# A tanh-gelu MLP in Strassen form: weight casts on another engine, sums of the next weights split over two pairs, one split and an input cast a pair later

## The chip, the cores and the metric

The kernel runs on one core of a Trainium2 chip. The metric is the device time of one execution in microseconds (us). A core has five engines that run side by side: TensorE (PE, the matmuls; its weight loads are shown as PEld), VectorE (DVE), ScalarE (ACT), GpSimd (POOL) and SyncE (SP). SP only issues transfers (DMA); POOL issues some as well. Each engine works through its own instructions in order, and semaphores tie the engines together. SBUF is the on-chip memory, PSUM the eight banks that PE writes to.

## What is computed

For x of 8 x 1024 x 1024, w1 of 1024 x 4096 and w2 of 4096 x 1024, all float32:

```python
h = x @ w1
h = 0.5 * h * (1 + np.tanh(np.sqrt(2 / np.pi) * (h + 0.044715 * h ** 3)))
return (h @ w2).astype(np.float32)
```

The kernel multiplies in float16 and adds up in float32.

## The kernel before

The rows of x are taken in eight blocks of 1024 (`sb` 0 to 7). For each block `matmul1` computes the hidden values with the gelu, and a second routine multiplies them by w2: `matmul2_made` for blocks 0 and 1, `matmul2` for the rest. Both products use Strassen's scheme in Winograd's form: each operand is cut in two by two blocks named "11", "12", "21" and "22", seven products replace eight, and some operands are sums of blocks. For the weights these are `W_SUM`: sum 5 is "12" less "11", 6 is "22" less sum 5, 7 is "22" less "12", 4 is "21" less sum 6. For x they are `S_SUM`, of which sums 5, 7, 6 and 3 are made in that order. DVE makes all of them (line 119, the helper `tt`).

`matmul1` runs over eight pairs of columns of hidden values, j = 0 to 7. In a pair, product 1 and product 2 come first, then the late product 4 of the pair before, then 5, 6, 3 and 7, each for two columns (h = 0, 1) with four matmuls per column, all at line 435. PSUM banks are copied to SBUF by ACT (`act_copy`, line 135), DVE adds another bank to the copy, ACT applies the gelu (line 448). A bank that takes a second product must have been copied first, and those copies stand on ACT in order with the gelus.

Most instructions are held in the order in which the program is written (`keep_in_program_order`), so the place of a call in these loops is its place in its engine's queue.

Weights of w1 come in quarters of four columns (class `MadeQuad`). In block 0 each is loaded in float32 by SP into a ring of four staging buffers (`gc`), cast to float16 (`raw`), summed, and stored for later blocks. POOL casts the second and later quarters (lines 138 and 213 to 226 for casts and stores). Pair 0 is special (class `First`): its columns are multiplied plainly in eight products, the second half of the rows in two parts of 256. Of the first quarter, DVE casts columns 0 and 1 (line 196), and POOL casts columns 2 and 3, for pair 1, with the same line. The loads and the casts of these are kept in `self.more`, and the casts are issued at the end of `pair`. The sums of x are made after each part (`sums`), and then `matmul1` makes the four weight sums for columns 2 and 3. At pair 1 the sums of the second quarter are `jobs`: `half` is how many of them run ahead of products 5 and 6 on DVE, and the rest run at the pair's end.

In block 1 the weight sums are made again, now with a further level: `split_in_m1` loads parts of w2's blocks 2 and 3 into two `gc` buffers, makes four sums in two more of them, and POOL stores these (`in_d`, line 841). The four splits are loaded at the end of pairs 0 to 3, and `matmul1` takes their sums into the jobs of the next pair. Also in block 1, `steady` casts the next block's x: POOL copies two elements of a gelu result as a mark (`pace`, line 412), and then issues two transfers that cast x rows to float16 in DRAM (`xb`, line 407). SP later loads `xb` transposed.

The second product of blocks 0 and 1 runs over four row groups for each of seven products, with 16 matmuls each (line 933). `FILL` says which sums DVE makes after which group. In block 0 the parts "12" and "22" of w2 are loaded in float32 to staged buffers and cast by ACT; POOL stores `in_d` (line 820) and the results (line 671).

Of the kernel before, what the change touches and what calls it, by code (L numbers as in the profile page):

```python
# [61 lines left out]
def kernel(  # L62
# [7 lines left out]
    nc = tc.nc  # L70
# [38 lines left out]
    def psum():  # L109
        return pp.tile([P, HT], F32, name="ps")  # L110
# [33 lines left out]
    def columns(t, c, n=1):  # L144

        h, c = divmod(c, 2)
        return t[:, h * KH:(h + 1) * KH, c * P:(c + n) * P]
# [11 lines left out]
    class MadeQuad:  # L159


        def __init__(self, q, first, store):
            self.q, self.first, self.store = q, first, store
            self.raw = {b: unit(2 * KH, 2 * P) for b in BLOCKS}
            self.ops = {m: self.raw[b] for m, b in W_TERM.items()}
            if not first:
                for b in ("12", "11", "22", "21"):
                    nc.sync.dma_start(out=flat(self.raw[b]), in_=raw_d[q][:, BLOCKS.index(b), :])
# [127 lines left out]
    def x_blocks():  # L296
        return {b: unit(KH, HT) for b in ("22", "21", "12", "11")}

    def keep_clock(bank, n):

        for _ in range(n):
            tc.keep_in_program_order(
                nc.tensor.matmul(bank, lhsT=idle[:, :P], rhs=idle, start=True, stop=True)
            )

    class First:


        def __init__(self):
            self.identity = consts.tile([P, P], DT, name="identity")  # L310
            make_identity(nc, self.identity)
            self.idle = psum()
            keep_clock(self.idle, 7)
            self.xs = XOps(x_blocks())
            self.rows = {}
            for q in range(NQ):
                self.load(0, q)
            self.quad = MadeQuad(0, True, False)
            casts = [self.quad.load_cols(b, 0, 2, nc.vector.tensor_copy) for b in range(2)]
            for q in range(NQ):  # L320
                self.load(1, q)
            for q in range(NQ):
                self.cast(0, q)
                self.transpose(0, q)
                keep_clock(self.idle, 2)
            for cast in casts:
                cast()
            self.more = [self.quad.load_cols(b, 2, 2, nc.gpsimd.tensor_copy) for b in range(2)]

        def load(self, a, q):  # L330
            r0 = a * HT + q * P
# [3 lines left out]
        def cast(self, a, q):  # L335
            xn = tp.tile([P, 2, HT], DT, name="tmp")
            tc.keep_in_program_order(nc.vector.tensor_copy(out=xn, in_=self.rows[a, q]))
            self.rows[a, q] = xn
# [21 lines left out]
        def pair(self, gelu):  # L360


            def plain(bank, a, b, c, part=None):
                cols = slice(None) if part is None else slice(part * HT // 2, (part + 1) * HT // 2)
                for r in (1, 2):
                    w = columns(self.quad.raw[f"{r}{b}"], c)
                    for k in range(KH):
                        tc.keep_in_program_order(nc.tensor.matmul(  # L368
                            bank[:, cols], lhsT=w[:, k, :], rhs=self.xs.blocks[f"{a}{r}"][:, k, cols],
                            start=r == 1 and k == 0 and not part,  # L370
                            stop=r == 2 and k == KH - 1,
                            skip_group_check=bool(part),
                        ))

            def sums(h):
                for m in (5, 7, 6, 3):
                    self.xs.make(m, cols=slice(h * HT // 2, (h + 1) * HT // 2), pin=True)

            for q in range(3):
                self.cast(1, q)  # L380
            for b, c in ((1, 0), (1, 1), (2, 0), (2, 1)):
                bank = psum()
                plain(bank, 1, b, c)
                if b == 2:
                    self.transpose(1, c)
                gelu(f"1{b}", c, bank)
            self.cast(1, 3)
            self.transpose(1, 2)
            banks = {(c, b): psum() for c in range(2) for b in (1, 2)}
            for part in range(2):  # L390
                for c in range(2):
                    for b in (1, 2):
                        plain(banks[c, b], 2, b, c, part)
                        if part:
                            gelu(f"2{b}", c, banks[c, b])
                    if c == 0 and not part:
                        self.transpose(1, 3)
                sums(part)
            for casts in self.more:
                casts()  # L400

    def x_cast(s, after, rows=range(0, SB, P), xb=None):
        if xb is None:
            xb = xdram.tile([SB, H], DT, name="xb")
        with tc.issue_after(after.ins):
            for q in rows:
                nc.gpsimd.dma_start(out=xb[q:q + P, :], in_=x2[s * SB + q:s * SB + q + P, :])
        return xb

    def x_cast_paced(s, g_chunk, q, xb):  # L410

        mark = nc.gpsimd.tensor_copy(out=pace, in_=g_chunk[:, :2])  # L412
        return x_cast(s, mark, range(q * P, (q + 2) * P, P), xb)

    def x_transpose(xb, dma, blocks=None, which=range(4)):
        blocks = blocks or x_blocks()
        for b, t in [list(blocks.items())[i] for i in which]:
            a, k = int(b[0]) - 1, int(b[1]) - 1
            for j in range(KH):
                dma(  # L420
                    t[:, j, :],
                    xb[a * HT:(a + 1) * HT, (k * KH + j) * P:(k * KH + j + 1) * P],
                    transpose=True,
                )
        return blocks
# [3 lines left out]
    def matmul1(xs, sb, quads, start=None):  # L429
        g = {b: gp.tile([P, NI, HT], GT, name=f"g{b}") for b in ("11", "12", "21", "22")}  # L430
# [68 lines left out]
        def ahead(j):  # L499

            if sb > 1 or j // 2 == NI // QC - 1:
                return ()
            q, second = divmod(j, 2)
            if not second:
                quad = MadeQuad(q + 1, sb == 0, sb == 1)
                quads.append(quad)
                if sb == 0:
                    quad.load()
                    quads[q].keep_raw()
            quad = quads[q + 1]  # L510
            if sb == 0:
                return [lambda m=m: quad.sum(m, pin=True) for m in SUMS] if second else ()
            jobs = [lambda m=m: quad.sum(m, pin=True) for m in ((7, 4) if second else (5, 6))]
            if sb == 1:
                if second:
                    jobs += [lambda m=m: quad.inner_sums(m) for m in INNER_1]
            return jobs

        def steady(j):

            if 0 < sb < NSB - 1:
                when = (0, 1, 2, 3) if sb > 1 else (4, 5, 6, 7)
                if j in when:
                    nxt["xb"] = x_cast_paced(sb + 1, g["11"][:, 2 * j + 1, :], 2 * when.index(j), nxt.get("xb"))
                if j == 3 and sb > 1:
                    nxt["blocks"] = x_blocks()
                if j > 3 and sb > 1:
                    x_transpose(nxt["xb"], load_in_order, nxt["blocks"], range(j - 4, j - 3))
            if sb > 1 and j == 5:
                early[7] = gcp.tile([P, NI // 2, HT // 2], GT, name="gc")  # L530
                u, v = (inner_block(g["22"], b) for b in ("11", "21"))
                nc.gpsimd.tensor_tensor(out=early[7], in0=u, in1=v, op=SUB)  # L532

        nxt, early = {}, {}
        splits = []
        late = None
        pending = []
        for j in range(NI // 2):
# [13 lines left out]
            jobs = list(ahead(j))  # L552
# [33 lines left out]
            difference(j - 1)  # L586
            half = (len(jobs) + 1) // 2
            if start is not None and j == 1:
                half = 0
            if sb == 1:  # L590
                half = 3 if j % 2 else 0
                jobs += splits
                splits = []
            for job in jobs[:half]:
                job()
            def six(h):
# [62 lines left out]
            if sb == 1 and j < 2 * len(SPLIT_IN_M1):  # L659
                splits = split_in_m1(SPLIT_IN_M1[j // 2], j % 2)  # L660
            steady(j)
        difference(NI // 2 - 1)
        blocks = nxt.get("blocks")
# [183 lines left out]
    def inner_block(t, b):  # L847
        a, k = int(b[0]) - 1, int(b[1]) - 1
        return t[:, k * NI // 2:(k + 1) * NI // 2, a * HT // 2:(a + 1) * HT // 2]
# [171 lines left out]
    for sb in range(NSB):  # L1021
        g, early, nxt = matmul1(xs, sb, quads, first if sb == 0 else None)
# [36 lines left out]
```

## Time and profile before

| what | value |
|---|---|
| median of 5 runs | 1495.36 us (1494.83 to 1498.94) |
| the profiled execution | 1496.6 us |
| its span, first to last instruction | 1494.8 us |
| PE busy in the span | 1480.8 us (99%) |
| DVE, ACT, POOL busy | 1155.3, 609.7, 235.3 us |
| granted PE clock, mean | 0.997 |
| POOL casts at line 196 | 4, mean 1148 ns |
| ACT casts of the same shape from SBUF (line 135) | 16, mean 1045 ns |
| DVE sums of 128x1024 f16 (line 119) | 52, mean 814 ns |
| DVE sums of 128x2048 f16 | 88, mean 1261 ns |
| block 0: first product, second product | to 119.1 us, to about 215.8 us |
| block 1: first product, second product | to 314.5 us, to about 411.4 us |

The times in the table are from one profiled execution, except for the median. A row of the profile names the engine, the line, the tile written and read, the shape, the count, and how long the engine was idle before it and what released it. "DMA share" is the mean busy share of the 16 DMA engines; it can go a little over 1. The granted clock is the share of full speed that PE is given.

### The profile page before, as it was taken

What the parts mean: (1) busy time and instruction counts of PE and PEld (TensorE: products, weight loads), DVE (VectorE), ACT (ScalarE), POOL (GpSimd) and SP (SyncE); (2) the same over time, 40 slices, a digit from 0 to 9 for tenths busy, and PEclk for the clock granted to TensorE, in tenths of its full rate; (3) what the DMA queues carried; (4) which work ended last, traced back from release to release, by engine and by line L of the source; (5) the groups of instructions that cost most, each with busy time, mean ns of one, the idle gap of its engine ahead of it and who ended that gap; (6) DMA issues with size and microseconds to landing.
All of it is one profiled execution on the core that took longest, in us unless ns stands there. A gap on an engine that the chain in (4) does not pass through costs nothing.

```text
span 1494.8 us, 26327 instructions
## 1 busy us (share of the span) xinstructions
PE 1480.8 (99%) x9879; PEld 965.3 (65%) x9879; DVE 1155.3 (77%) x1792; ACT 609.7 (41%) x1146; POOL 235.3 (16%) x314
## 2 busy tenths in 40 slices
PE   8999999999999999999999999999999999999998
PEld 4444444444455788557875588755886568855687
DVE  6756548757767899778987799877997779877787
ACT  4566116531066411663126631366214652156510
POOL 3552022312311011110121001210011101101011
PEclk9999999999999999999999999999999999999999
DMA  9999996997997999999999899998999999997886
GB/s 331 329 342 395 261 339 224 384 286 246 345 318 183 327 296 309 333 225 367 305 323 315 226 381 311 303 321 241 358 297 315 309 262 339 294 367 243 293 282 214
DMA packets 242719, 453.70 MB, mean 304 GB/s; under 512 B 80672, under 2 KB 85792, under 8 KB 241696
## 3 DMA queue, kind: packets, MB, share of 16 engines
q1 hardware_dynamic: 215680, 358.69, 71.4%
q0 software_dynamic: 26912, 93.34, 21.3%
q8 instruction: 77, 1.26, 0.3%
q14 instruction: 50, 0.41, 0.1%
HBM read 355.47 MB, written 111.15 MB: 312 GB/s over the span
## 4 chain that ended last, share of the span: by engine, by line
PE 86%; issue 7%; DMA 3%; DVE 2%; POOL 2%; ACT 0%; POOLq 0%; DVEq 0%; ACTq 0%
PE ps L435 44%; PE ps L892 34%; PE ps L933 7%; DVE tmp L119 1%; DVE u L119 1%; DMA in_d<-gc 1%; DMA u<-in_w_dram 1%; PE ps L368 1%; DMA xb<-in_x_dram 1%; POOL out_dram L671 0%; POOL w_d L213 0%; POOL in_d L841 0%; PE ps L345 0%; DMA u<-in_x_dram 0%; POOL in_d L226 0%
## 5 line engine op out<-in xcount | busy, mean ns | idle before, releaser
L435 PE MATMUL ps<-u 128*128 128x512 f16 (+1 forms) x4104 | 750.0, 345 | 7.7 <-DVE u L119 3.5
L119 DVE TENSOR_TENSOR tmp<-tmp,ps 128x256 f32<-128x256 f32 (+1 forms) x930 | 450.6, 532 | 267.0 <-PE ps L435 174.3
L435 PEld LDWEIGHTS <-u 128*128 128x128 f16 x4104 | 402.0, 98 | 353.2 <-issue 17.5
L135 ACT COPY tmp<-ps 128x512 f32<-128x512 f32 x410 | 231.8, 582 | 309.3 <-PE ps L435 157.3
L448 ACT ACTIVATE g<-tmp 128x512 f16<-128x512 f32 x378 | 238.3, 633 | 170.6 <-DVE tmp L119 170.5
L892 PE MATMUL ps<-u,gc 128*128 128x256 f16 x2688 | 300.4, 273 | 0.0
L892 PEld LDWEIGHTS <-gc 128*128 128x128 f16 x2688 | 262.5, 98 | 31.2
L119 DVE TENSOR_TENSOR u<-u 128x2048 f16<-128x2048 f16 (+3 forms) x292 | 224.8, 809 | 16.8 <-DMA in_d<-u 7.3
L892 PE MATMUL ps<-u,g 128*128 128x256 f16 x2016 | 227.9, 273 | 0.0
L135 ACT COPY u<-ps 128x512 f32<-128x512 f32 (+1 forms) x134 | 78.0, 587 | 348.8 <-PE ps L892 341.3
L892 PEld LDWEIGHTS <-g 128*128 128x128 f16 x2016 | 197.3, 98 | 24.1
L683 POOL DMA_DIRECT2D out_dram<-u x70 | 64.1, 982 | 710.1 <-issue 365.7
L119 DVE TENSOR_TENSOR u<-u,ps 128x512 f32<-128x512 f32 x216 | 147.8, 684 | 34.6 <-PE ps L892 28.8
L933 PE MATMUL ps<-u,g 128*128 128x512 f16 x768 | 166.4, 379 | 0.0
L933 PEld LDWEIGHTS <-g 128*128 128x128 f16 x768 | 75.1, 98 | 90.7
L119 DVE TENSOR_TENSOR g<-g,g 128x2048 f16<-128x2048 f16 (+1 forms) x136 | 130.7, 983 | 1.6 <-ACT g L448 1.6
L119 DVE TENSOR_TENSOR gc<-g,gc 128x2048 f16<-128x2048 f16 x84 | 102.4, 1219 | 0.6
L119 DVE TENSOR_TENSOR gc<-g 128x2048 f16<-128x2048 f16 x78 | 95.0, 1219 | 0.0
L448 ACT ACTIVATE g<-ps 128x512 f16<-128x512 f32 x134 | 80.1, 598 | 16.1 <-PE ps L435 6.9
L138 POOL CAST u<-gc 128x1024 f16<-128x1024 f32 x40 | 49.9, 1262 | 37.7 <-DMA gc<-in_w_dram 27.9
L412 POOL COPY pace<-g 128x2 f16<-128x2 f16 x24 | 5.5, 229 | 198.2 <-ACT g L448 198.2
L532 POOL TENSOR_TENSOR gc<-g 128x2048 f16<-128x2048 f16 x6 | 24.4, 4067 | 61.9 <-ACT g L448 61.9
(35 smaller groups left out, 252.2 us busy)
## 6 DMA issues: line engine op xcount, KB each, us to landing
u<-w_d SPq DMA_DIRECT2D x336, 256.0 KB, 6.4
u<-in_d SPq DMA_DIRECT2D x168, 512.0 KB, 7.0
u<-raw_d SPq DMA_DIRECT2D x252, 256.0 KB, 7.2
out_dram<-u POOLq DMA_DIRECT2D x70, 512.0 KB, 9.4
gc<-in_w_dram SPq DMA_DIRECT2D x48, 512.0 KB, 5.8
u<-in_d SPq DMA_DIRECT2D x96, 256.0 KB, 6.6
raw_d<-u SPq DMA_DIRECT2D x32, 512.0 KB, 10.1
u<-raw_d SPq DMA_DIRECT2D x32, 512.0 KB, 11.6
```

What stands on the lines that cost most here:

```text
L119: i = nc.vector.tensor_tensor(out=out, in0=in0, in1=in1, op=op)
L135: tc.keep_in_program_order(nc.scalar.copy(out=out, in_=in_))
L138: pool_last[0] = nc.gpsimd.tensor_copy(out=out, in_=in_)
L368: tc.keep_in_program_order(nc.tensor.matmul(bank[:, cols], lhsT=w[:, k, :], rhs=self.xs.blocks[f"{a}{r}"][:, k, cols], start=r == 1 and k ...
L412: mark = nc.gpsimd.tensor_copy(out=pace, in_=g_chunk[:, :2])
L435: tc.keep_in_program_order(nc.tensor.matmul(bank, lhsT=w, rhs=x, start=first and k == 0, stop=k == n - 1, skip_group_check=not first,))
L448: gelu_last[0] = nc.scalar.activation(out=g[b][:, c, :], in_=src, func=GELU)
L532: nc.gpsimd.tensor_tensor(out=early[7], in0=u, in1=v, op=SUB)
L683: return nc.gpsimd.dma_start(out=rows, in_=src, **kw)
L892: tc.keep_in_program_order(nc.tensor.matmul(bank[:, i * OH // 2:(i + 1) * OH // 2], lhsT=t[:, c, i * P:(i + 1) * P], rhs=self.y[j][:, c, : ...
L933: tc.keep_in_program_order(nc.tensor.matmul(pair(bank), lhsT=a[:, c, :], rhs=chunks(pieces[c // QC])[:, :, c % QC, :], start=(first and c ...
```

## The change

There are four edits.

1. The casts of columns 2 and 3 of the first quarter go from POOL to ACT. They are issued in two groups: two in part 0 behind the plain products of column 1, which puts them on ACT after the copies of the transposes and before the first gelus of pair 0's second half; two in part 1 behind the gelus of column 0. Before, they were issued at the end.
2. At pair 1 of block 0 only sums 5 and 6 of the second quarter are made at the pair's end. Sums 7 and 4 run in pair 2, ahead of its products 5 and 6 in the written order.
3. In block 1 the sums of the last split are not taken at pair 4 but at pair 5; as `half` is 3 there, they run at that pair's end.
4. In block 1 the four pieces of the x cast go from pairs 4, 5, 6, 7 to pairs 5, 6, 7, 7.

```diff
-            self.more = [self.quad.load_cols(b, 2, 2, nc.gpsimd.tensor_copy) for b in range(2)]
+            self.more = [self.quad.load_cols(b, 2, 2, nc.scalar.copy) for b in range(2)]
...
                     if c == 0 and not part:
                         self.transpose(1, 3)
+                    if part != c:
+                        self.more[part]()
                 sums(part)
-            for casts in self.more:
-                casts()
...
-                when = (0, 1, 2, 3) if sb > 1 else (4, 5, 6, 7)
-                if j in when:
-                    nxt["xb"] = x_cast_paced(sb + 1, g["11"][:, 2 * j + 1, :], 2 * when.index(j), nxt.get("xb"))
+                when = (0, 1, 2, 3) if sb > 1 else (5, 6, 7, 7)
+                for q in range(4):
+                    if when[q] == j:
+                        nxt["xb"] = x_cast_paced(sb + 1, g["11"][:, 2 * j + 1, :], 2 * q, nxt.get("xb"))
...
             if start is not None and j == 1:
-                half = 0
+                half, jobs, rest = 0, jobs[:2], jobs[2:]
+            elif start is not None and j == 2:
+                half, jobs = 2, rest
             if sb == 1:
                 half = 3 if j % 2 else 0
-                jobs += splits
-                splits = []
+                if j != 4:
+                    jobs += splits
+                    splits = []
```

In the built program PE's and SP's instructions keep their order. ACT has four more, POOL four fewer.

## The prediction

> **What bounds the kernel now.** First the busy shares: TensorE (PE) is busy for 1480.8 us of the span of 1494.8, so only its holes and its slow stretches can be won. The list of who waited for whom, cut to PE, gives the holes of the long run (line, what it waited for: us in total, times, longest):
>
> ```profile
> PE ps L435 <- DVE u L119: 3.5, 1, 3.5
> PE ps L435 <- ACT tmp L135: 2.5, 2, 1.8
> PE ps L435 <- DVE tmp L119: 1.7, 6, 0.3
> ```
>
> The third row is six times 0.3 in the later blocks of x, which the change leaves alone. The first is one hole of 3.49 us (30.79 to 34.28), the second two holes, 0.70 (53.64 to 54.34) and 1.80 (284.15 to 285.94). The view by stretches shows a further loss after the first (stretch, its length, busy us and count of PE, weight loads, DVE, ACT, POOL, then granted clock, DMA share, GB/s):
>
> ```profile
> 27.00:31.00 4.00, 3.79 (x20) 1.62 (x17) 3.86 (x4) 1.86 (x4) 3.67 (x3) 1.00 0.92 319
> 31.00:34.30 3.30, 0.02 (x1) 0.02 (x2) 3.19 (x3) 0.00 (x0) 2.84 (x3) 0.82 1.01 340
> 36.00:38.00 2.00, 2.00 (x6) 0.73 (x5) 2.00 (x3) 0.59 (x1) 1.24 (x2) 0.50 0.92 306
> 40.00:44.00 4.00, 4.00 (x21) 1.78 (x19) 0.61 (x1) 1.32 (x3) 0.60 (x1) 1.00 1.03 395
> 284.00:286.00 2.00, 0.20 (x2) 0.06 (x1) 2.00 (x5) 1.21 (x3) 0.93 (x2) 1.00 0.99 399
> ```
>
> In the first hole the clock falls to 0.50 and stays there until 39.96: 5.68 us of matmuls at half speed, 2.84 lost. The 1.80 us hole does not lower it. All that can be won is 3.49 + 2.84 + 0.70 + 1.80 = 8.83 us.
>
> Next, what is late before each hole. The timeline of the first (start, length, engine, operation, count, idle before):
>
> ```profile
> 20.94 1.04 POOL L196 CAST u<-gc 128x1024 f16<-128x1024 f32 x1 [19.63 <-DMA gc<-in_w_dram]
> ...
> 23.44 14.27 DVE L119 TENSOR_TENSOR u<-u 128x1024 f16<-128x1024 f16 x11 [0.28 <-PE ps L368]
> ...
> 28.05 2.75 POOL L138 CAST u<-gc 128x1024 f16<-128x1024 f32 x2
> ...
> 34.28 19.36 PE L435 MATMUL ps<-u 128*128 128x512 f16 x76 [3.49 <-DVE u L119]
> ```
>
> Eleven sums take 14.27 us, 1.3 each, while the one at 22.48, with no cast on POOL, takes 0.68. PE waits for the ninth of the twelve, the first weight sum (ends 34.23). The middle hole:
>
> ```profile
> 280.20 1.42 DVE L119 TENSOR_TENSOR gc<-gc 128x1024 f16<-128x1024 f16 x2 [1.16 <-DMA in_d<-gc]
> 282.86 1.29 DVE L119 TENSOR_TENSOR gc<-gc 128x1024 f16<-128x1024 f16 x2 [1.25 <-DMA in_d<-gc]
> 284.07 1.28 DVE L119 TENSOR_TENSOR tmp<-tmp,ps 128x512 f32<-128x512 f32 x2
> 285.94 28.73 PE L435 MATMUL ps<-u 128*128 128x512 f16 x132 [1.80 <-ACT tmp L135]
> ```
>
> Split sums wait for buffers whose stores land 13.2 us after issue; the adds behind them are late, then the gelu on ACT behind an add, then the copy behind that gelu, which PE needs.
>
> **The change part by part.** *Casts to ACT.* Removed from POOL: four casts, mean 1148 ns. Added to ACT: four; the nearest row is ACT's own cast of 128x1024 f32 to f16 from SBUF, 1045 ns (16 of them), so 4.2 us. Data land at 20.9, 23.8, 25.3 and 26.7 (issue plus landing). ACT is free at 22.50: casts 22.5 to 23.5 and 23.8 to 24.9; gelus at 24.9 and 25.6 as before; casts 26.2 to 27.2 and 27.2 to 28.2; then the gelus of 26.50 and 27.37 at 28.2 and 28.7, two copies to 30.4. PE needs those copies for product six, at 33 us: 2.6 us of cover. The pool behind the casts' buffers gets its first one 1.5 us later, the third 0.8 later; SP's loads are queued behind each other anyway (the load of 22.00 lands after 6.0 us, that of 25.06 after 4.2), so I count nothing, with 0 to 1.5 us of lateness for the range.
>
> *DVE without them.* POOL is now idle until the next quarter's first cast (28.05). The sums wait for PE twice (23.4 and 26.9); so sum six of the second half starts at 27.7. From there two more sums with a POOL cast between each: 1.41 each as in the rows of 24 to 34 us, at best 0.69. 28.45 + 1.41 + 1.41 gives 31.3 for the first weight sum, at best 29.9. PE is through with its 16 matmuls at 30.79: hole 0.6 (0 to 1.2) for 3.49. No fall of the clock then. Here "SBUF — State Buffer", Who interferes with whom, speaks against the change: of a DVE instruction with two SBUF inputs and a POOL one that reads SBUF, the second blocks until the first is through. With a cast of 1.04 that is up to 1.73 a sum, so 31.9 and a hole of 1.1. I take the row's 1.41.
>
> *What is late next.* Three weight sums follow (0.69 to 1.41 each, with two casts arriving): until 34.9; the add to 35.5; gelu 0.63, copy 0.59 to 36.7. PE, running from 31.4 at 0.216 (64.91 us by 300), has done five, six and half of three, 20 matmuls, at 35.7. A second hole of about 1.0 (0 to 1.2), hidden before by the half clock. Then 12 matmuls to 39.3. Before, the same point is 34.28 + 13 x 0.427 + 19 x 0.216 = 43.9. Won so far: 4.6.
>
> *Sums of the next quarter over two pairs.* Nothing is added. Before, four sums (46.05 to 52.55, 2.05 us each where POOL casts) stand ahead of the adds of pair 2 and make the 0.70 hole. After, two stand there (1.22 each, at worst 2.05, from 40.8 on, done by 45) and two behind the adds; product seven needs its sum at 49, done by 48.5. Won: 0.70. What queues behind the two are the adds of p5, not due earlier. Together 5.3.
>
> *How much of it lasts.* Casts and loads of the first block run by their own DMA loop (share 0.9 to 1.06). The sums of the second weight matrix in the first block are where that shows:
>
> ```profile
> 136.29 1.29 DVE L119 TENSOR_TENSOR u<-u 128x1024 f16<-128x1024 f16 x2 [7.34 <-DMA in_d<-u]
> 136.57 1.04 ACT L135 CAST u<-u 128x1024 f16<-128x1024 f32 x1 [2.83 <-DMA u<-in_w_dram]
> ...
> 144.97 1.22 DVE L119 TENSOR_TENSOR u<-u 128x2048 f16<-128x2048 f16 x1
> ```
>
> The four sums "5" end at 140.45, 141.59, 144.46 and 146.19; PE (128 matmuls after 119.09, then one piece each 0.86) reads them at 146.7, 147.6, 148.4 and 149.3. The last has 3.1 us of slack. It need not be fixed: DVE's adds and the in_d store move with PE, but each sum takes over the buffer of a staged load, cast on ACT until 141.65. That gives at best 141.65 + 1.22 plus the adds between, 144.5: PE may come 4.8 us earlier. Against this stands "DMA: Bandwidth & Descriptors", Queues, rings and completion order: each DMA engine serves its queue rows in turn. The fourth POOL store (137.88), 5 us earlier, would go between SP's loads; 512 KB at 402 GB/s is 1.3 us: 3.5 by the rule. The trace has both kinds: POOL's stores there land after 8.3 us, SP's loads after 14.6. I keep 4.8, with 3.1 as the low end.
>
> *Split and x cast later.* Four split sums (0.69 each) go from the end of pair 4 to that of pair 5, the x cast's pieces a pair later, two at pair 7; four POOL stores and eight x DMAs keep their number. By 293 the stores that held the buffers (issued until 269.6, 13.2 us) have long landed, so the sums run through as at the end of pair 3 (266.70, 2.62 us, no hole behind). Won: 1.80 (0 if they still wait). SP's transposes of x wait for the last pieces: 310.2 + 6.2, say 3 us later for two more pieces; their blocks are read after 411. In POOL's queue the split's four stores now stand behind pair 5's weight stores and its x piece; what they write is read in the third block of x, past 500 us; but they must free buffers for the first sums of the next product at 314: 296 + 13.2 = 309, earlier still with PE.
>
> **Sum.** 4.8 + 1.8 = 6.6 us off the profiled span: 1488.2. That execution took 1496.6, 1.8 around its span and 1.2 above the median of 1495.36, which goes to **1488.8 us**.
>
> **Rivals.** *DMA order gives part back* (the rule above): head 3.1, sum 4.9, 1490.5. For it: share 1.04 at 120 to 140. *The first hole stays*, since eight quarter casts on POOL meet the sums, the clock falls again: head 0.5 to 1, with the middle 2.5, 1492.9. Against it: POOL has nothing before 28. *The middle hole only moves* to pair 6: 4.8, 1490.6. Against it: pair 3. *Slower:* ACT frees the load buffers later (1.5 us for the first); if that loop, on four buffers, falls behind by d until the second product, PE loses d at 146 us. The 3.1 us of slack and the 1.8 of the middle are used up at d = 4.9; at d = 8 it is 1498.5. Against it: DMA has room at 48 to 58 us (190 GB/s at 49.4 to 54.4) to catch up.
>
> **How the numbers follow.** Main case 0.52, DMA order 0.17, hole moves 0.08, first hole stays 0.11, slower 0.12. What measurement tells from no change is 0.2%, 3 us. Faster: the first three and half of the fourth, 0.82; within: the other half and a little of the last, 0.08; slower 0.10. Range: from all 8.83 won, 1486.5, to 1493.5, which leaves out the slower case and part of the fourth; the main case alone is 1487.5 to 1490.
>
> **What would show it.** Waits of PE: the DVE row under 1.2 and the clock at 1.00 throughout 31 to 40 us; ACT's row at about 1 us, near 36, none at 284. Sums of 128x1024 before 28 us at 0.69. PE's second product starting at about 114; from there a hole at 141 to 145 would say how much is given back. The prediction is wrong if ACT's casts start later than 22.5 and 26.2, if DVE's sums cost 1.4 without POOL's casts, or if PE waits for DVE at 140 to 160 by more than 2 us.

## The result, and the profile after

| | before | after |
|---|---|---|
| median | 1495.61 us (41 executions, 1493.28 to 1498.94) | 1492.15 us (21 executions, 1490.37 to 1495.35) |
| the profiled execution | 1496.6 us | 1490.69 us |
| its span | 1494.8 us | 1488.9 us |
| mean granted clock in it | 0.997 | 0.999 |

The ratio is 0.9977, with an interval of 0.9971 to 0.9983: 3.5 us faster, where 6.6 were forecast. The two profiled executions differ by more, 5.9 us. That gap is the main question of what follows.

The waits of PE, as before (line, what it waited for: us in total, times, longest):

```profile
PE ps L435 <- DVE tmp L119: 1.9, 7, 0.3
PE ps L937 <- DVE u L119: 1.6, 2, 0.8
...
PE ps L435 <- ACT tmp L135: 0.6, 1, 0.6
```

The wait of 3.5 us on the first weight sum is gone, and so are the two on ACT's copies (53.64 and 284.15 before). The 0.6 us of ACT's row are a new wait, at 35.18. New is also the second row: two waits on sums in block 0's second product (line 937 is the former 933).

The stretches of the first hole and of the half clock (stretch, length, busy us and count of PE, weight loads, DVE, ACT, POOL, then granted clock, DMA share, GB/s):

```profile
27.00:31.00 4.00, 4.00 (x22) 1.96 (x21) 3.81 (x5) 3.13 (x6) 2.41 (x2) 1.00 0.85 254
31.00:34.30 3.30, 3.30 (x17) 1.49 (x16) 3.30 (x4) 0.59 (x1) 1.48 (x2) 1.00 0.88 254
36.00:38.00 2.00, 2.00 (x11) 0.94 (x10) 0.26 (x1) 1.19 (x3) 1.90 (x3) 1.00 1.00 358
```

PE is busy through all three, at clock 1.00: 11 matmuls from 36 to 38 us, where there were six. The timeline of the same place shows why (start, length, engine, operation, count, idle before):

```profile
22.47 1.05 ACT L196 CAST u<-gc 128x1024 f16<-128x1024 f32 x1
...
23.91 1.05 ACT L196 CAST u<-gc 128x1024 f16<-128x1024 f32 x1 [0.40 <-DMA gc<-in_w_dram]
...
26.20 1.98 ACT L196 CAST u<-gc 128x1024 f16<-128x1024 f32 x2
27.01 6.95 DVE L119 TENSOR_TENSOR u<-u 128x1024 f16<-128x1024 f16 x7 [0.75 <-PE ps L368]
...
27.25 7.93 PE L435 MATMUL ps<-u 128*128 128x512 f16 x36
27.95 1.38 POOL L138 CAST u<-gc 128x1024 f16<-128x1024 f32 x1 [26.64 <-DMA gc<-in_w_dram]
...
35.74 1.46 PE L435 MATMUL ps<-u 128*128 128x512 f16 x6 [0.56 <-ACT tmp L135]
```

ACT casts where the prediction put it. POOL's first cast starts at 27.95; DVE's seven sums from 27.01 take 0.99 us each, the eleven before took 1.30. PE runs from 27.25 to 35.18 without a hole. In the middle, the sums of the last split now run through, and PE does not wait:

```profile
271.79 18.51 PE L435 MATMUL ps<-u 128*128 128x512 f16 x85
...
285.48 2.62 DVE L119 TENSOR_TENSOR gc<-gc 128x1024 f16<-128x1024 f16 x4
```

And this is block 0's second product, where some of the head's gain is lost again:

```profile
140.58 1.99 ACT L135 CAST u<-u 128x1024 f16<-128x1024 f32 x2 [1.89 <-DMA u<-in_w_dram]
...
141.66 1.23 DVE L119 TENSOR_TENSOR u<-u 128x2048 f16<-128x2048 f16 x1
...
142.94 1.02 PE L937 MATMUL ps<-u,g 128*128 128x512 f16 x4 [0.84 <-DVE u L119]
...
143.40 1.22 DVE L119 TENSOR_TENSOR u<-u 128x2048 f16<-128x2048 f16 x1
...
144.67 5.56 PE L937 MATMUL ps<-u,g 128*128 128x512 f16 x25 [0.71 <-DVE u L119]
```

ACT was idle 1.89 us until a load landed, then cast, then DVE summed, and PE had to wait for two sums. In this execution PE came to the second product at 112.58 (before: 119.09), 6.5 us earlier, and left it at 211.14 (before: 215.78), 4.6 us earlier. With the middle, PE is 6.7 us earlier at 412, and 5.9 at the end.

### The profile page after: what moved, and what is told of

The parts are those of the page before. It is cut to its first block, busy times and chain, and to the rows that moved or that the text cites. A ratio compares the mean times of both kernels' runs of the same rounds, so it can differ in the third digit from the quotient of the medians.

```text
span 1488.9 us, 26324 instructions
## 1 busy us (share of the span) xinstructions
PE 1478.1 (99%) x9879; PEld 964.4 (65%) x9879; DVE 1147.9 (77%) x1792; ACT 613.0 (41%) x1150; POOL 223.7 (15%) x310
## 4 chain that ended last, share of the span: by engine, by line
PE 94%; DMA 3%; DVE 2%; issue 0%; ACT 0%; DVEq 0%; SPq 0%; ACTq 0%
PE ps L435 48%; PE ps L896 35%; PE ps L937 11%; DMA u<-in_w_dram 1%; DVE tmp L119 1%; DMA raw_d<-u 1%; PE ps L368 1%; DVE u L119 0%; PE ps L345 0%; DMA u<-in_x_dram 0%; ACT tmp L135 0%; DMA u<-xb 0%; ACT u L135 0%; PE ps L303 0%; ACT g L448 0%
## 5 line engine op out<-in xcount | busy, mean ns | idle before, releaser
L119 DVE TENSOR_TENSOR u<-u 128x2048 f16<-128x2048 f16 (+3 forms) x292 | 217.7, 784 | 25.2 <-ACT u L135 10.3
L138 POOL CAST u<-gc 128x1024 f16<-128x1024 f32 x40 | 44.1, 1105 | 70.0 <-DMA gc<-in_w_dram 57.4
```

The source lines that it names most:

```text
L119: i = nc.vector.tensor_tensor(out=out, in0=in0, in1=in1, op=op)
L138: pool_last[0] = nc.gpsimd.tensor_copy(out=out, in_=in_)
```

## The experiments

All medians are of 11 or 12 executions unless said. The runs stand in the order in which they explain each other; the first eight were made in two sets, with 1495.41 and 1495.66 us for the kernel before (35 executions each).

### The parts by themselves

Head edits only: casts on ACT, and sums over two pairs.

```diff
-            self.more = [self.quad.load_cols(b, 2, 2, nc.gpsimd.tensor_copy) for b in range(2)]
+            self.more = [self.quad.load_cols(b, 2, 2, nc.scalar.copy) for b in range(2)]
...
+                    if part != c:
+                        self.more[part]()
...
-                half = 0
+                half, jobs, rest = 0, jobs[:2], jobs[2:]
+            elif start is not None and j == 2:
+                half, jobs = 2, rest
```

> Only the casts on ScalarE and the sums over two pairs; the x cast and the split stay as before. Theory (the prediction's steps): block 0's second product starts about 6.5 us earlier than before, about 1.5 us of that is given back at 142 to 145 us by two sums that come too late, so about 4.9 us come off the span; the hole of 1.80 us at the second m1 (284.15 before, now about 279) stays. Rival (the parts help each other): less than 4 us, because the later x cast is needed to keep the give-back at 1.5.

Measured: 1494.33 us, ratio 0.9993 (0.9984 to 1.0002). At most 2.4 us are won, most likely 1. In its profile PE comes to the second product at 113.21, 5.9 us earlier than before, so the head itself is as fast as expected. But the waits in that product (now line 935) are 3.0 us:

```profile
PE ps L935 <- DVE u L119: 3.0, 3, 1.8
...
PE ps L435 <- ACT tmp L135: 1.8, 1, 1.8
```

and it is left at 213.41. The last row is the untouched hole in block 1's first product, which the expectations call the second m1. Casts only:

```diff
-            self.more = [self.quad.load_cols(b, 2, 2, nc.gpsimd.tensor_copy) for b in range(2)]
+            self.more = [self.quad.load_cols(b, 2, 2, nc.scalar.copy) for b in range(2)]
...
+                    if part != c:
+                        self.more[part]()
```

> Only the casts on ScalarE. Theory: the first hole goes and the clock stays 1.00 behind it; the hole of 0.70 us at pair 2 (53.64 before) stays. If block 0's second product caps what of the head's gain lasts, as the prediction says, the span still falls by about 4.9 us, as in the kernel with both head edits: the give-back at 142 to 145 is 0.7 us smaller. Rival (no cap, a fixed loss): 4.2 us, with the same give-back of 1.5.

Measured: 1494.8 us, ratio 0.9996 (0.9987 to 1.0004). PE comes to the second product at 112.96 and there is no hole at pair 2, against the expectation: once the first weight sums are early, the four sums of the next quarter end in time by themselves. In the traces the casts do all of the head's work (113.21 was no earlier). What is given back, 2.6 us (the product takes 99.29 against 96.69 before), is between those of the other kernels with this head, so it tells nothing of a cap or a fixed loss. Sums over two pairs only:

```diff
-                half = 0
+                half, jobs, rest = 0, jobs[:2], jobs[2:]
+            elif start is not None and j == 2:
+                half, jobs = 2, rest
```

> Only the next quarter's sums over two pairs. Theory: the 0.70 us hole at pair 2 goes, the first hole and the half clock stay, no hole at 142 to 145, since a head that is 0.7 us shorter is well within the slack: 0.7 us off the span. Rival: nothing, because pair 1's sums then come in the way of its weights.

Measured: 1495.44 us, ratio 1.0001 (0.9992 to 1.0009): no gain to be seen. The hole at pair 2 is gone in its profile, but it has a hole that nobody expected of it, in the second product:

```profile
PE ps L435 <- DVE u L119: 2.5, 1, 2.5
PE ps L435 <- ACT tmp L135: 2.2, 1, 2.2
...
PE ps L935 <- DVE u L119: 1.3, 1, 1.3
```

The second row is the hole in block 1's first product. This head has the old casts on POOL, and still PE waits 1.31 us at 160.25 for the last of the sums "6"; the last load of block "22" landed at 159.2 in this execution. So the second product can hold PE up in kernels without the change too. The middle edits only (the split, and the x cast a pair later):

```diff
-                jobs += splits
-                splits = []
+                if j != 4:
+                    jobs += splits
+                    splits = []
...
-                when = (0, 1, 2, 3) if sb > 1 else (4, 5, 6, 7)
-                if j in when:
-                    nxt["xb"] = x_cast_paced(sb + 1, g["11"][:, 2 * j + 1, :], 2 * when.index(j), nxt.get("xb"))
+                when = (0, 1, 2, 3) if sb > 1 else (5, 6, 7, 7)
+                for q in range(4):
+                    if when[q] == j:
+                        nxt["xb"] = x_cast_paced(sb + 1, g["11"][:, 2 * j + 1, :], 2 * q, nxt.get("xb"))
```

> Only the split of the second m1 and the x cast a pair later; the casts stay on VectorE. Theory: the hole at 284.15 goes and nothing else, 1.8 us off the span; the first hole of 3.49 us and the clock of 0.50 behind it stay, and there is no hole at 142 to 145. Rival: nothing is won, because the wait moves to the next product.

(The casts that this text puts on VectorE are on GpSimd, as in the kernel before.) And the split without the x cast:

```diff
-                jobs += splits
-                splits = []
+                if j != 4:
+                    jobs += splits
+                    splits = []
```

> Only the last split of the second m1. Theory: it alone removes the hole at 284.15, 1.8 us off the span; the x cast a pair later is worth nothing. Rival: the x cast stands in the way at that place and the hole only shrinks.

Measured: 1495.18 us, ratio 0.9990 (0.9980 to 1.0000), and 1493.17 us, 0.9984 (0.9975 to 0.9992). The intervals hold 1.8 us (0.9988) both, and the traces are plain: with either kernel PE is busy throughout the place of the hole, here in the one with the split alone:

```profile
280.00:292.00 12.00, 12.00 (x58) 5.38 (x57) 10.78 (x20) 7.48 (x14) 4.38 (x9) 1.00 0.99 372
```

From the end of the second product to the same matmul late in the second block (418.80 before) PE takes 203.02 us before, 200.97 with both middle edits and 200.98 with the split alone. The split is worth 2.05 us of the trace, the x cast nothing.

### The clock by itself

The kernel before, with 15 matmuls of idle data put into the first hole (into the bank that product five of pair 1 overwrites):

```diff
+                    if start is not None and j == 1 and h == 0:
+                        keep_clock(banks_c[0], 15)
                     product(banks_c[h], source, 5, cs[h], True)
```

> The kernel before, with 15 dummy matmuls put into the first hole on TensorE and nothing else. Theory: the clock stays 1.00 through 31 to 40 us, so about 2.8 us come off the span although the wait for the first weight sum is the same; the give-back is nothing, since 2.8 is inside the slack of 3.1 us. Rival: the product behind the hole was held by its data and not by the clock; nothing is won.

Measured: 1496.56 us, ratio 1.0002 (0.9994 to 1.0011): no gain. The timeline of PE shows that the head did gain:

```profile
31.30 3.40 PE L303 MATMUL ps<-idle 128*128 128x512 f16 x15
34.71 4.49 PE L435 MATMUL ps<-u 128*128 128x512 f16 x20
40.12 2.10 PE L435 MATMUL ps<-u 128*128 128x512 f16 x9 [0.92 <-ACT tmp L135]
```

20 matmuls take 4.49 us, full clock, although the hole before them is as long as before. A wait of 0.92 follows, and PE comes to the second product at 116.97, 2.1 us earlier than in the profile of before. In the median nothing of that is left; 2.8 us lie outside the interval. The second product did not take it back in this trace: PE goes through it without a wait. Two things on record bear on it. The granted clock of every execution is known: of 94 of the kernel before in the four sets of runs, 31 had 1.000 as a mean, which by its rounding leaves at most 1.5 us at 0.50; 35 had 0.999 and 28 less. The profiled one had 0.997, and only 11 of the 94 were as low. So the long half clock that the dummies remove is missing from many executions. With the dummies 9 of 11 had 1.000, yet their median is no better than that of the 31 (1494.97). And the dummies last 3.40 us, while three other profiles with the old casts have a first hole of 2.53 to 2.76: there they would hold PE up. No profile shows such an execution, so the cause stays open.

### The changed kernel again, and what the second product does

> The changed kernel again, for a second profile beside the other kernels of this set on one chip: the holes of 0.56 us near 35 and of 1.5 us together at 142 to 145 are there again if they belong to the kernel and not to the one execution; median 3 to 4 us under the kernel before.

No edit. Measured: 1492.68 us, ratio 0.9985 (0.9977 to 0.9994). Its profile differs from the first one of the same kernel just where the question lies. The waits of PE:

```profile
PE ps L937 <- DVE u L119: 3.1, 3, 1.8
...
PE ps L435 <- DVE u L119: 0.5, 1, 0.5
```

PE's timeline in the second product:

```profile
143.22 1.02 PE L937 MATMUL ps<-u,g 128*128 128x512 f16 x4 [0.53 <-DVE u L119]
144.95 11.38 PE L937 MATMUL ps<-u,g 128*128 128x512 f16 x52 [0.71 <-DVE u L119]
...
160.77 1.46 PE L937 MATMUL ps<-u,gc 128*128 128x512 f16 x6 [1.84 <-DVE u L119]
```

The two waits at 142 to 145 are there again, 1.24 us together, and a third of 1.84 at 158.93, for the last sum "6". That sum waits for ACT's cast of the eighth load of "22", which landed at 158.4:

```profile
158.41 1.05 ACT L135 CAST u<-u 128x1024 f16<-128x1024 f32 x1 [6.14 <-DMA u<-in_w_dram]
...
159.49 1.23 DVE L119 TENSOR_TENSOR u<-u 128x2048 f16<-128x2048 f16 x1 [8.31 <-ACT u L135]
```

In the first profile it had landed at 155.7, and the sum came 0.47 us in time. The hole near 35 belonged to the one execution: here PE waits 0.51 us for the first weight sum at 31.27, and nowhere else from there to the second product. Six other profiles with these casts have the same 0.38 to 0.51, and none of them a second hole.

Put beside each other, with all profiles of kernels whose stores stand as before (start and end of block 0's second product on PE, in us; 96.69 is its length without a wait; its end is the start of the next matmul behind it):

| kernel | start | length | end |
|---|---|---|---|
| before | 119.09 | 96.69 | 215.78 |
| middle edits only | 119.90 | 96.69 | 216.59 |
| split only | 118.25 | 96.69 | 214.94 |
| dummies for the clock | 116.97 | 96.69 | 213.66 |
| sums only | 116.06 | 98.16 | 214.23 |
| changed kernel, first | 112.58 | 98.57 | 211.14 |
| changed kernel, again | 113.17 | 100.25 | 213.43 |
| head edits only | 113.21 | 100.20 | 213.41 |
| casts only | 112.96 | 99.29 | 212.25 |
| block 0's x cast later (next) | 112.99 | 101.53 | 214.52 |

The starts spread over 7 us, the ends over 5, for the early starters take longer. The five with ACT's casts start at 112.98 on average and give back 3.28. The profile that the prediction was compared with is the best of these five.

The loads that the product waits for do not follow PE. The first of the eight "22" loads landed at 136.6 in the kernel before and at 135.3, 135.3, 136.4 and 134.4 in four of those five. From 130 to 140 us the stretch of before reads:

```profile
130.00:140.00 10.00, 10.00 (x48) 4.49 (x46) 3.71 (x5) 3.63 (x5) 1.08 (x2) 1.00 1.04 393
```

and that of after:

```profile
130.00:140.00 10.00, 10.00 (x49) 4.48 (x47) 5.53 (x7) 3.30 (x5) 1.08 (x2) 1.00 1.04 392
```

DMA share 1.04 in both, though PE is 6.5 us further on in the second.

### Whose place in the queue it is

First the transfers that POOL issues there. The changed kernel, with block 0's x cast later:

```diff
-                if (m, q) == (2, 1) and sb == 0:
-                    xb = x_cast(sb + 1, at[1])
+                if (m, q) == (2, 3) and sb == 0:
+                    xb = x_cast(sb + 1, at[3])
```

> The changed kernel, with block 0's x cast for the next block issued one more step later, behind the third step of the pair. Theory of the queue order (the loads of the 22 staged weights for block 0's second product land late because GpSimd's x transfers share the DMA engines with them): those loads land up to 1.5 us earlier, the holes at 142 to 145 shrink, 0.5 to 1.5 us off the changed kernel's span. Rival (the loads are late because the whole stream of loads is paced by the buffers that come free, not by GpSimd's transfers): the holes stay at 1.5 us together and the time is the changed kernel's.

Measured: 1492.29 us, ratio 0.9977 (0.9968 to 0.9987), as the changed kernel. The theory that these transfers delay the first "22" loads fell: in this execution the first landed at 139.9, later than in any other, and the loads of "12" ahead of it were late already at 117.7 (115.5 in the changed kernel), long before the moved transfers are issued. PE's waits in the second product are 4.2 us, more than without the move. But the eighth load landed at 150.2, after 12.0 us in flight; in the two profiles of the changed kernel, where POOL's transfers of x are issued while it is in flight, it took 21.0 and 24.3.

Then SP's own queue. In the changed kernel four stores stand ahead of the "22" loads (a row of SPq is a run of transfers that SP issues: start of the first, time to the end of the last issue, count):

```profile
115.49 4.39 SPq L132 DMA_DIRECT2D raw_d<-u  x4
120.95 15.73 SPq L132 DMA_DIRECT2D u<-in_w_dram  x8
136.73 27.03 SPq L132 DMA_DIRECT2D raw_d<-u  x12
```

They keep w2's block "11" in float16 for the later blocks. The edit puts them behind:

```diff
         bring("12", act_copy, True)
-        keep("11")
         if sb:
             bring("22", None, False)
...
                     bring("22", act_copy, True)
-                    for b in ("21", "12", "22"):
+                    for b in ("11", "21", "12", "22"):
                         keep(b)
```

> The changed kernel, with the four stores of the quarters 11 of the second weight matrix (4 x 512 KB, raw_d<-u, issued 115.5 to 119.6) put behind the eight loads of the quarters 22 in SP's queue, where the other twelve stores already stand. Theory (what lasts of the head's gain is capped by the stream of transfers, whose loads of the quarters 22 land at a fixed time whatever TensorE does): 2 MB at 400 GB/s is 5.2 us, so the first four of those loads land near 130 to 136 and not 135 to 141, the last before 150; the holes at 140 to 161 go, and the median falls by a further 2 to 3.5 us, to 1489 to 1490.5. Rival (the spread lies elsewhere): the same median as the changed kernel, 1492 to 1493. Second rival: the stores, now later, delay the transposes of x behind them and a new hole opens after 165.

Measured: 1490.65 us (5 executions), ratio 0.9966 (0.9954 to 0.9979), just above the 1489 to 1490.5 expected. The same edit on the kernel before:

> The kernel before, with the same four stores moved. Theory: its TensorE comes to the second product of the first block some 6 us later, so the cap binds it little; 0 to 1.5 us faster than before, by those executions in which a late load made a hole there. Rival (the stores cost the kernel time by themselves, whatever the head does): as much gain as in the changed kernel, 2 to 3.5 us.

Measured: 1495.25 us, ratio 0.9998 (0.9989 to 1.0007). In its profile PE comes to the second product at 116.89, and that of the changed kernel with the same stores moved at 113.83: 3.1 us apart, not 6. And the first of the two once more:

> The changed kernel with the four stores of the quarters 11 behind the loads of the quarters 22 a second time, for more executions. Theory of the cap: the median lies again 2 us or more under the changed kernel's (1492.2 to 1492.7), at 1489.5 to 1491, and the holes at 140 to 147 are gone. Rival (the first five executions were lucky): 1492 or more.

Measured: 1489.2 us (5 executions, 1488.83 to 1493.79), ratio 0.9967 (0.9955 to 0.9980). The ten executions of both have a median of 1490.42. In SP's timeline of the first, the loads run on behind those of "12", and the sixteen stores follow:

```profile
114.78 15.11 SPq L132 DMA_DIRECT2D u<-in_w_dram  x9
130.76 33.12 SPq L132 DMA_DIRECT2D raw_d<-u  x16
164.83 1.65 SPq L132 DMA_TRANSPOSE u<-xb  x1
```

DVE's timeline of the same kernel has the last two sums "6" that PE is to read:

```profile
151.25 1.22 DVE L119 TENSOR_TENSOR u<-u 128x2048 f16<-128x2048 f16 x1 [2.84 <-DMA raw_d<-u]
157.55 1.23 DVE L119 TENSOR_TENSOR u<-u 128x2048 f16<-128x2048 f16 x1 [5.08 <-DMA raw_d<-u]
```

and PE's timeline:

```profile
137.78 17.65 PE L936 MATMUL ps<-u,g 128*128 128x512 f16 x81
...
158.83 3.40 PE L936 MATMUL ps<-u,gc 128*128 128x512 f16 x15 [0.81 <-DVE u L119]
```

The "22" loads landed from 130.7 to 141.5 (before the edit 135.3 to 155.7). PE goes through 140 to 155 without a hole, where it had two, and keeps one of 0.81 at 158.02: sums "6" are written over block "11" and now wait for its stores. The transposes of x behind the stores start at 164.83, before at 164.76, so nothing is lost there. The product takes 97.66 and 97.96 us in the two profiles and ends at 211.49 and 211.15. The second profile has holes of 0.38 at 143.56 and 0.57 at 157.92, so the first of the old holes is smaller there (1.2 and 1.6 us for the two before) and not gone. Its eight "22" loads have landed by 140.2, and DVE works without a break from 135.81 to beyond that hole: what PE waits for there is DVE's own order. In time, the stores bring the changed kernel some 2 us (0.9966 and 0.9967 against 0.9977 and 0.9985, intervals that touch), and the kernel before nothing (0.9998). With the holes that shrank or went, this shows the cause of some 2 us: what of the head's gain lasts is set to that extent by when these loads land. With the old head they are mostly in time: of its five profiles with the stores in the old place one has a wait there, 1.31 us.

Last, both moves together, to see what holds the fourth store:

```diff
-                if (m, q) == (2, 1) and sb == 0:
-                    xb = x_cast(sb + 1, at[1])
+                if (m, q) == (2, 3) and sb == 0:
+                    xb = x_cast(sb + 1, at[3])
...
-        keep("11")
...
-                    for b in ("21", "12", "22"):
+                    for b in ("11", "21", "12", "22"):
```

> The same with block 0's x cast for the next block issued behind (2, 3) and not (2, 1). In the profile of the kernel with the stores moved one hole was left, 0.81 us at 158.02: the last sum 6 waited for the fourth of these stores, in flight from 134.82 to 157.43 beside GpSimd's eight transfers of x (issued 140.1 to 146.3). Theory (those transfers hold it up): that store lands before 152, the hole goes, up to 0.8 us less than with the stores alone. Rival: the store is held up by something else and nothing changes.

Measured: 1489.33 us (5 executions, 1488.6 to 1492.14), ratio 0.9966 (0.9952 to 0.9979), the time of the stores alone; the span of its profile is the shortest of all, 1487.3. The hole at 158 is gone, one of 0.43 at 143.06 is left:

```profile
PE ps L936 <- DVE u L119: 0.4, 1, 0.4
```

The fourth store was in flight from 134.18 to 146.85, 12.7 us, where it had taken 22.6. With the eighth load above (12.0 against 21.0 and 24.3), that makes two cases in which the x transfers hold up what SP has in flight beside them. Here it is worth the hole of 0.6 to 0.8 us at 158, which the times do not resolve. With the stores moved, both kernels are faster than the changed one; between them nothing is decided.

## Why the prediction was right or wrong

The forecast, 1488.8 us, lies 3.4 us under the measured median: inside the range given, outside the main case's own 1487.5 to 1490. The 6.6 us of the sum are nearly twice the 3.5 measured; that the time fell inside is owed to a range that reached up to 1493.5. The first case, with 4.8 us of the head lasting, is not what the typical execution does. Of the signs that the prediction named as its refutation one appeared: PE waits for DVE at 140 to 160 us for 1.6 us in the first profile of the changed kernel, under the 2 us named, and for 3.1 in the second.

*Casts to ACT.* Right to a tenth: 22.47, 23.91, 26.20 and 27.13 for 22.5, 23.8, 26.2 and 27.2, 1.05 us each.

*DVE without them.* Right: a hole of 0.6 was expected, 0.38 to 0.51 is there in seven profiles and none in the first one. There only one of the two sums with a POOL cast beside it took 1.41, the other 0.68. The 1.73 us of full blocking that the prediction weighed show nowhere: the longest such sum from 22 to 40 us takes 1.53 in any profile. The clock stayed at 1.00 behind it in all.

*What is late next.* A second hole of 1.0 near 36 was expected. It was 0.56 in the one profile without a first hole, and in the others there was none. No profile has both, so it seems to be one lateness that shows at one place or the other; the step counted both.

*Sums over two pairs, won 0.70.* Wrong. The kernel with the casts alone has no hole at pair 2, and the sums alone moved no median. With an early head there was no hole left to win, as the second product's start shows too: 113.21 with the sums, 112.96 without. A late head does not always make it either: the kernel before with the stores moved has its first hole (2.65 us) and none at pair 2. The head's gain was 6.5 us against the profile of before, 5.3 expected; but three other profiles with the old head started the second product at 119.90, 118.25 and 116.89, so 5.5 is the fairer number (118.5, the mean of these three and before, less 112.98).

*How much of it lasts, 4.8.* This step was mis-sized. The first profile agreed (4.64), the others did not: 2.4, 2.4, 3.5 and 1.3 against the profile of before, and by the medians of the head edits 1.1 us and of the casts alone 0.6. The mechanism was named, the sums "5" and the loads that they need. But the slack of 3.1 us and the cast's end at 141.65 were read off one execution and taken as fixed, and the sums "6" were not looked at, of which the last has 0.47 us of slack in one execution of the changed kernel and is 1.84 us late in the next. Over the profiles with the stores in the old place the eighth "22" load landed anywhere from 147.4 to 159.2. The rule that I weighed there and set aside, from the Trainium skill, "DMA: Bandwidth & Descriptors", Queues, rings and completion order (each DMA engine serves its queue rows in turn), came nearer in number: that rival had 3.1 us and 1490.5. Its own mechanism, POOL's earlier `in_d` stores between SP's loads, was not tested, so that is in part luck; the rule fits POOL's x transfers, beside which SP's took 21 to 24 us and not 12 to 13. The runs with the stores moved show what I had not seen: some 2 us come from SP's own row, from four stores ahead of the loads.

*Split and x cast later.* Right: 1.80 expected, 2.05 in the traces, by the split alone, and nothing from the x cast.

*The sum.* It was made from the profiled span and then lowered by the 1.2 us by which that execution lay above its median. Against the profiled span it holds: 1490.0 expected for such an execution, 1490.69 and 1492.49 measured. The step to the median took off too much. Four profiles with the old head differ by 3.0 us in when the second product starts, so part of what made that execution long was head, and the change removes that same head; to subtract it again counts it twice. The granted clocks say the same: the 2.84 us of half clock in the prediction belong to an execution at 0.997; the 11 executions of the kernel before at 0.997 or less have a median of 1497.8 us, the 31 at 1.000, which by their clock lost at most 0.75 us so, 1495.0. How much of the missing 3.1 us this is, no run isolates. In the medians 0.6 to 1.1 us come from the head (the interval of the larger reaches from nothing to 2.4), and 1.8 to 2.05 from the middle in the traces, 2.4 to 3.2 together; 3.0 and 3.5 were measured.

Of the rivals, the slower one (load buffers freed later by ACT) left no trace: the last of the "gc" loads landed at 114.0 after and 114.5 before.

What stays open is what makes the stream of transfers differ from one execution to the next. By 120 us the profiles have moved between 40.1 and 41.2 MB, which is 2.7 us at 402 GB/s. The least belongs to the kernel whose first "22" load was the latest, but the late eighth loads are not ordered by it (40.5 MB, 40.8 and 41.2 for those of 159.2, 158.4 and 157.2). Open is also where 7 of 33 executions of the changed kernel, up to 1495.35 us long, lost clock to 0.998 or less; neither of its two profiles shows a fall before the end, and none of its 15 executions with the stores moved went so low.

## What to carry to other kernels

Before adding up what a hole gives, find the next place where PE meets data that come at their own time, and take the slack there from several executions, for every kind of sum and not only the first. Where a stretch is filled by transfers, an earlier engine gains only as far as the last needed load; look in that load's own queue for stores that nobody needs yet and put them behind. A gain measured between two profiles is not the gain of the medians: here 5.9 against 3.5. Before a loss of one profile goes into the sum, see from what is known of every execution, here the granted clock, how many of them have it.

## What was not expected of the hardware

Shorter holes than the first one lower the clock too. Holes of 2.53, 2.65 and 2.76 us (the kernels with the sums only, with the stores moved on the kernel before, and with the split only) were followed by a clock of 0.50, though it fell only after PE had begun again, and for about 3.4 us; that of 3.49 us was followed by 6.8 us. The stretches of the kernel with the stores moved on the kernel before, whose hole ended at 33.99:

```profile
34.00:36.00 2.00, 2.00 (x6) 0.78 (x7) 1.97 (x2) 0.31 (x1) 2.00 (x2) 0.56 1.01 376
36.00:38.00 2.00, 2.00 (x7) 0.72 (x6) 2.00 (x2) 0.28 (x1) 2.00 (x3) 0.59 0.93 222
38.00:40.00 2.00, 2.00 (x11) 0.87 (x9) 2.00 (x4) 1.11 (x3) 1.16 (x1) 1.00 0.98 363
```

A hole of 2.23 us (282.59, sums only) and those of 1.7 to 1.8 did not lower it. The Trainium skill, "TensorE: Matmul & The Clock Gate", Why this matters for your kernels, allows gaps up to about 3 us; three of these are shorter and were followed by a fall. If the length of the hole alone decides, which no run tests, the limit lay between 2.2 and 2.5 in these few cases. And a clock kept high by idle work was worth nothing in the median time.
